# Expert selections in pieces, one to a slot of rows, and one head further ahead

## The chip, the cores and the metric

The kernel runs on one core of a Trainium2 chip. The metric is the device time of one execution in microseconds; lower is better. TensorE (PE) multiplies, VectorE (DVE) and ScalarE (ACT) do elementwise work, GpSimd (POOL) issues the indirect DMAs that gather rows by index, and SyncE (SP) issues the loads of weights. Each engine works through its own queue in order.

## What is computed

A two-layer diffusion backbone on 256 latent and 256 context tokens, 1024 wide, float32. Each layer has a token mixer (projections, windowed and differential attention, convolution, pooling, four gated branches) and then a feed-forward part that looks up experts (PEER). The change touches only the second:

```
q  = (h @ wq)                                  # 128 tokens, 8 heads, 2 x 128
s1, s2 = q[:, :, 0] . k1, q[:, :, 1] . k2      # 128 scores each
v1, i1 = top_k(s1, 16);  v2, i2 = top_k(s2, 16)
cand   = v1[:, None] + v2[None, :]             # 16 x 16 sums
sc, ci = top_k(cand, 16)
idx    = i1[ci // 16] * 128 + i2[ci % 16]      # 16 of 16384 experts
gate   = softmax(sc)
act    = gelu(sum_d h * u_tab[idx])
out    = sum over 8 heads, 16 experts: gate * act * v_tab[idx]
```

For each tile of 128 tokens that is 8 heads x 16 slots, and each slot fetches one row of u_tab and one of v_tab for each token: 128 x 1024 floats, 0.5 MB, twice. The last layer needs only the latent tiles, so there are six tiles to gather: layer 0 context tile 0, latent tiles 2 and 3, context tile 1, then layer 1 latent tiles 2 and 3.

## The kernel before

The kernel is written with a tile framework. Its build has a scheduler: the order in which the Python code writes instructions is their priority, and the scheduler puts an instruction into its engine's queue when, by its own estimates, its inputs and its buffers are ready and the engine is free. A lower priority can so pass a higher one that isn't ready yet. The queues are fixed when the kernel is built.

`gather(t, on_dve, nxt, side)` is a generator that does one tile. It has nine rounds `h` of 16 slots `k`. A slot issues `u_slot` (row of u for head `h`, line 1124 on POOL; product and sum on DVE, line 1132) and `v_slot` (row of v for head `h - 1`; added up on DVE, line 1149, or on TensorE, line 1156, with a diagonal made by ACT). A round ends with `weigh(h)`: Gelu on ACT (line 1138) and a product with the gate on DVE (line 1139). Row places are rings: five tiles for u, five for v, and more that `lend` adds where other buffers are free.

`select` finds the 16 experts of one head for one or two tiles (jobs): `top16` of each half of the scores (lines 1011 to 1015), the sums `cand` (1040), `top16` of these, the softmax (Exp on ACT, line 1049), the lookup through `df` (1060) and `pk` (1063), and `idx` (1064). Its tiles mx, ix, cand, sv, ci, pk have one buffer each. `route` is what comes before: it loads the head's w_q (1 MB, a ring `w` of three places that all weights share, line 231) and kt (one place), multiplies (line 218, then 1196 for the scores) and has ACT copy the scores to `sc` (1199).

`router` yields once for each head. `gather` takes one step of `side` ahead of each round, so that head `h + 1` is routed and selected, in one go, ahead of the slots of round `h`. Three gathers have such a `side`:

- the first gather (context tile 0, POOL issues from 410 to 985 us) runs `behind` the main work on the latent tiles; `pump` puts slots between the main work's pieces at fixed rates. Its side is `router((0, 1), ...)`, one tile per selection; the scores of tile 1 are written to `later` in DRAM.
- the second gather (tile 2, 1001 to 1404) runs alone, with `router((2, 3), ...)`, two tiles per selection.
- the third gather (tile 3, 1405 to 1782) runs alone, with `waited`, which reads the scores of tile 1 back and selects two heads at a time.

The fourth gather (context tile 1, 1784 to 2257) runs behind layer 1's main work and has no side. The fifth (2376 to 2783) begins behind the last of it and has `routes` as its side, which yields twice and then does heads 3 to 7; heads 0 to 2 are routed in the main code. The sixth (2784 to 3149) runs alone.

## Time and profile before

| | |
|---|---|
| median of 3 runs | 3176.56 us (3165.32 to 3186.99) |
| the profiled execution | 3168.74 us, span 3167.0 us |
| TensorE busy | 2376.9 us (75%) |
| VectorE busy | 2357.8 us (74%) |
| GpSimd busy | 1789.3 us (56%) |
| ScalarE busy | 654.6 us (21%) |
| read from HBM | 1032.22 MB, 327 GB/s over the span |

A share of the span is an average over the six gathers and the main work. Which engine or which transfers set the pace is to be read stretch by stretch. A wait is put down to what was released last; where that engine had long been done, it was something else, often the release of a buffer.

### The profile page before, as it was taken

What the parts mean: (1) busy time and instruction counts of PE and PEld (TensorE: products, weight loads), DVE (VectorE), ACT (ScalarE), POOL (GpSimd) and SP (SyncE); (2) the same over time, 40 slices, a digit from 0 to 9 for tenths busy, and PEclk for the clock granted to TensorE, in tenths of its full rate; (3) what the DMA queues carried; (4) which work ended last, traced back from release to release, by engine and by line L of the source; (5) the groups of instructions that cost most, each with busy time, mean ns of one, the idle gap of its engine ahead of it and who ended that gap; (6) DMA issues with size and microseconds to landing.
All of it is one profiled execution on the core that took longest, in us unless ns stands there. A gap on an engine that the chain in (4) does not pass through costs nothing.

```text
span 3167.0 us, 32196 instructions
## 1 busy us (share of the span) xinstructions
PE 2376.9 (75%) x10264; PEld 1586.2 (50%) x10264; DVE 2357.8 (74%) x5204; ACT 654.6 (21%) x1543; POOL 1789.3 (56%) x1542
## 2 busy tenths in 40 slices
PE   7999989898877785665455589899997966645555
PEld 5879878666666452222111267667696522211111
DVE  5977679678968899747666769977567985566666
ACT  3454321233112211110000211123332211100001
POOL 0000057443556687776777757766205777777775
PEclk9999999899988897886777789899998988876767
DMA  9948979787999899998999999999838989999998
GB/s 305 334 161 285 304 263 351 270 296 250 339 331 356 321 392 364 336 381 294 373 369 369 338 343 389 341 388 386 300 107 288 323 324 372 372 344 372 383 377 300
DMA packets 397863, 1036.48 MB, mean 327 GB/s; under 512 B 30464, under 2 KB 169216, under 8 KB 397696
## 3 DMA queue, kind: packets, MB, share of 16 engines
q0 software_dynamic: 221184, 805.40, 68.0%
q1 hardware_dynamic: 173072, 226.25, 21.0%
q10 hardware_dynamic: 3440, 2.78, 0.3%
q8 instruction: 82, 1.34, 0.2%
q14 instruction: 85, 0.70, 0.1%
HBM read 1032.22 MB, written 2.10 MB: 327 GB/s over the span
## 4 chain that ended last, share of the span: by engine, by line
PE 33%; DVE 18%; issue 17%; DMA 15%; POOL 15%; ACT 1%; another core or an unknown queue 0%; POOLq 0%; SPq 0%; ACTq 0%; DVEq 0%
PE mm L218 11%; POOL u L1124 8%; POOL v L1124 7%; DMA v<-in_v_dram,idx 7%; DVE u L1132 5%; PE va L1156 4%; DMA w<-in_w_gate_dram 3%; PE mm L214 3%; PE mm L216 2%; PE mm L215 2%; PE mm L916 2%; DMA u<-in_u_dram,idx 2%; DVE dacc L1149 2%; PE at L531 2%; DVE m L832 2%
## 5 line engine op out<-in xcount | busy, mean ns | idle before, releaser
L1124 POOL DMA_INDIRECT u<-in_u_dram,idx x768 | 869.7, 1132 | 926.4 <-DVE m L862 409.0
L1156 PE MATMUL va<-v,dg 128*128 128x512 f32 x1436 | 890.5, 763 | 554.5 <-DMA v<-in_v_dram,idx 379.8
L1132 DVE SCALAR_TENSOR_TENSOR u<-u,h 128x1024 f32<-128x1024 f32 x768 | 933.2, 1219 | 338.1 <-DMA u<-in_u_dram,idx 307.6
L1124 POOL DMA_INDIRECT v<-in_v_dram,idx x768 | 919.1, 1197 | 433.6 <-issue 193.9
L1156 PEld LDWEIGHTS va<-v,dg 128*128 128x128 f32 x1436 | 315.8, 237 | 1070.4 <-issue 925.6
L1149 DVE SCALAR_TENSOR_TENSOR dacc<-v,wt,dacc 128x1024 f32<-128x1024 f32 x403 | 515.6, 1279 | 105.9 <-DMA v<-in_v_dram,idx 78.6
L218 PE MATMUL mm<-hT,w 128*128 128x256 f32 (+1 forms) x1664 | 383.4, 385 | 71.4 <-DMA w<-in_w_gate_dram 50.9
L218 PEld LDWEIGHTS mm<-hT,w 128*128 128x128 f32 x1664 | 312.4, 207 | 130.2 <-issue 53.6
L1154 ACT ACTIVATE dg<-ident,wt 128x128 f32<-128x128 f32 x359 | 141.3, 400 | 1029.9 <-PE va L1156 524.7
L832 DVE SCALAR_TENSOR_TENSOR m<-m,cols,m 128x256 f32<-128x256 f32 x360 | 158.2, 473 | 0.1
L916 PE MATMUL mm<-hT,w 128*128 128x256 f32 x512 | 134.5, 405 | 14.5 <-DVE t L453 6.6
L215 PE MATMUL mm<-hT,whi 128*128 128x256 f32 x512 | 143.4, 280 | 0.0
L214 PE MATMUL mm<-hT,whi 128*128 128x256 f32 x448 | 128.0, 286 | 3.1 <-ACT whi L176 3.1
L216 PE MATMUL mm<-hT,whi 128*128 128x256 f32 x448 | 127.2, 284 | 1.8 <-DVE whi L177 1.8
L218 PE MATMUL mm<-w,hT 128*128 128x256 f32 x512 | 117.1, 388 | 10.6 <-DMA w<-in_w_in_dram 10.6
L916 PEld LDWEIGHTS mm<-hT,w 128*128 128x128 f32 x512 | 97.6, 202 | 34.5 <-issue 17.2
L177 DVE TENSOR_TENSOR whi<-w,whi 128x1024 fp32r<-128x1024 f32 x86 | 103.6, 1220 | 13.8 <-ACT whi L176 6.5
L218 PEld LDWEIGHTS mm<-w,hT 128*128 128x128 f32 x512 | 99.1, 195 | 26.4 <-issue 12.5
L176 ACT CAST whi<-w 128x1024 fp32r<-128x1024 f32 x86 | 87.4, 1047 | 51.3 <-PE mm L216 20.6
L215 PEld LDWEIGHTS mm<-hT,whi 128*128 128x128 f32 x512 | 97.0, 190 | 0.4 <-issue 0.3
L214 PEld LDWEIGHTS mm<-hT,whi 128*128 128x128 f32 x448 | 85.3, 190 | 8.8 <-ACT whi L176 4.2
L216 PEld LDWEIGHTS mm<-hT,whi 128*128 128x128 f32 x448 | 84.8, 189 | 7.2 <-DVE whi L177 3.7
(361 smaller groups left out, 2960.9 us busy)
## 6 DMA issues: line engine op xcount, KB each, us to landing
w<-in_w_gate_dram SPq DMA_DIRECT2D x48, 1024.0 KB
w<-in_w_in_dram SPq DMA_DIRECT2D x42, 1024.0 KB
X<-in_w_mod_dram SPq DMA_DIRECT2D x40, 512.0 KB
wm<-in_w_mod_dram SPq DMA_DIRECT2D x40, 512.0 KB
w<-in_w_branch_dram SPq DMA_DIRECT2D x20, 1024.0 KB
w<-in_w_q_dram SPq DMA_DIRECT2D x20, 1024.0 KB
u<-in_u_dram,idx POOLq DMA_INDIRECT x768
v<-in_v_dram,idx POOLq DMA_INDIRECT x768
```

What stands on the lines that cost most here:

```text
L177: nc.vector.tensor_tensor(lo.bitcast(FR), v, hi, op=OP.subtract)
L214: nc.tensor.matmul(ps, ah, bh, start=first, stop=False)
L215: nc.tensor.matmul(ps, ah, bl, start=False, stop=False)
L216: nc.tensor.matmul(ps, al, bh, start=False, stop=last)
L218: nc.tensor.matmul(ps, a[:, kb, ca], b[:, kb, cb], start=first, stop=last)
L832: nc.vector.scalar_tensor_tensor(acc[:, b, :], yb[:, b, k:k + T], cols[:, l, cw + k:cw + k + 1], acc[:, b, :], op0=OP.mult, op1=OP.add)
L916: nc.tensor.matmul(ps, a[:, kb, ca], b[:, k0 + kb, cb], start=f, stop=z, skip_group_check=True)
L1124: nc.gpsimd.indirect_dma_start(out=r, out_offset=None, in_=table, in_offset=bass.IndirectOffsetOnAxis(ap=self.idx[:, j:j + 1], axis=0))
L1132: nc.vector.scalar_tensor_tensor(r, r, 1.0, self.h2, op0=OP.mult, op1=OP.mult, accum_out=self.act[:, j % 16:j % 16 + 1])
L1149: nc.vector.scalar_tensor_tensor(self.dacc, v, w, self.dacc, op0=OP.mult, op1=OP.add)
L1154: nc.scalar.activation(dg, ident, AF.Copy, scale=w)
L1156: nc.tensor.matmul(self.va[:, half, :], dg, v[:, half * 512:(half + 1) * 512], start=j == self.pe[0], stop=j == self.pe[-1])
```

## The change

`select`, `route` and `waited` become generators that yield 0 after a piece and 1 at the end of a head. `gather` takes steps until the first 1 ahead of round 0 (that is head 1), and then one step ahead of each slot until the next 1; what a round has not used up is done at its end. So round `h` now selects head `h + 2`. `at_once` runs a generator through where the selection is done in one go as before. For two tiles a head has ten steps, for one tile seven. In `routes` head 3 is done at once, in round 1; its `lend` follows as soon as a head is done.

```
 def select(jobs, scs):
...
         for j, sc in enumerate(scs):
             for b in range(2):
                 top16(sc[:, b * 128:(b + 1) * 128], mx[:, 2 * j + b], ix[:, 2 * j + b])
+                yield 0
...
         for j in range(J):
             top16(cand[:, j].rearrange("p a b -> p (a b)"), sv[:, j], ci[:, j])
+            yield 0
...
+        yield 0
         nc.vector.tensor_reduce(pk, df, axis=AX.X, op=OP.min, apply_absolute_value=True)
...
 def route(ts, l, h, hT, c0, later=None, w=None):
...
+        yield 0
+        yield 0
         if jobs:
-            select(jobs, scs)
+            yield from select(jobs, scs)
+
+    def at_once(steps):
+        for _ in steps:
+            pass
...
 def router(tiles, l, ts, later=None, beside=None):
...
             if i == 0:
-                route(ts[:1], l, 0, hT, 0, later)
+                at_once(route(ts[:1], l, 0, hT, 0, later))
...
         for h in range(1, 8):
-            route(ts, l, h, hT, 0, later)
+            yield from route(ts, l, h, hT, 0, later)
             yield 1
-        route(ts[1:], l, 0, hT, 128, later)
+        yield from route(ts[1:], l, 0, hT, 128, later)
         yield 1
...
 def waited(t, later):
...
-            select([(t, h), (t, h + 1)], scs)
+            yield from select([(t, h), (t, h + 1)], scs)
...
 def gather(t, on_dve, nxt=None, side=()):
...
         side = iter(side)
         t.begin(on_dve)
+        while not next(side, 1):
+            pass
         for h in range(9):
-            next(side, None)
             if h == 8:
                 t.gates()
+            over = False
             for k in range(16):
+                if not over:
+                    over = next(side, 1)
                 if h < 8:
                     t.u_slot(h * 16 + k)
                 if h > 0:
                     t.v_slot(h * 16 - 16 + k)
                 yield 1
+            while not over:
+                over = next(side, 1)
             if h < 8:
                 t.weigh(h)
...
         for h in range(3, 8):
-            route(tsl, 1, h, hT, 0, w=wq[h] if h < len(wq) else None)
+            steps = route(tsl, 1, h, hT, 0, w=wq[h] if h < len(wq) else None)
+            if h == 3:
+                at_once(steps)
+            else:
+                yield from steps
             lend(**freed.get(h, {}))
             yield 1
```

The other calls of `route` in layer 1's main code are wrapped in `at_once`.

## Rows read from the trace of the kernel before

**Rows 1.** Busy time of each engine in stretches, TensorE clock, DMA share, GB/s.

```profile
core 0: us, PE busy (x) PEld busy (x) DVE busy (x) ACT busy (x) POOL busy (x), PEclk, DMA share, GB/s
395.00:985.00 590.00, 505.60 (x2358) 411.79 (x2358) 479.05 (x1072) 134.46 (x318) 317.82 (x256) 0.92 0.86 306
420.00:550.00 130.00, 119.14 (x556) 102.68 (x554) 121.86 (x265) 18.89 (x39) 91.53 (x66) 0.97 0.92 329
550.00:985.00 435.00, 364.56 (x1676) 289.60 (x1677) 342.55 (x748) 106.37 (x252) 220.47 (x185) 0.90 0.85 306
1097.00:1303.00 206.00, 145.28 (x387) 74.06 (x385) 205.42 (x685) 36.60 (x86) 163.16 (x134) 0.84 0.98 369
1493.00:1764.00 271.00, 145.52 (x193) 46.64 (x192) 178.81 (x247) 20.46 (x54) 207.41 (x193) 0.72 0.98 372
1500.00:1550.00 50.00, 25.67 (x36) 8.58 (x36) 35.33 (x51) 3.03 (x8) 38.11 (x40) 0.78 1.03 407
2484.00:2590.00 106.00, 81.23 (x263) 46.18 (x263) 105.58 (x334) 22.64 (x53) 77.03 (x65) 0.90 0.89 314
```

**Rows 2.** Line 1064 in three stretches: count, ns, first and last start.

```profile
L1064 DVE SCALAR_TENSOR_TENSOR idx<-pk x8: 156/165/168, 409.1 to 875.1; 128x16 int32<-128x16 f32 x8
...
L1064 DVE SCALAR_TENSOR_TENSOR idx<-pk x13: 163/186/221, 1000.7 to 1295.3; 128x32 int32<-128x32 f32 x11, 128x16 int32<-128x16 f32 x2
...
L1064 DVE SCALAR_TENSOR_TENSOR idx<-pk x10: 154/175/228, 2375.1 to 2589.7; 128x32 int32<-128x32 f32 x6, 128x16 int32<-128x16 f32 x4
```

**Rows 3.** Line 1139, ends of the second gather's eight rounds, 990 to 1400.

```profile
L1139 DVE TENSOR_TENSOR wt<-wt,gate x8: 152/168/176, 1055.7 to 1389.2; 128x16 f32<-128x16 f32 x8
```

**Rows 4.** POOL in order of time; in brackets idle time before, and releaser.

```profile
451.83 1.86 POOL L1124 DMA_INDIRECT v<-in_v_dram,idx  x1 [7.54 <-DVE idx L1064]
...
507.75 1.68 POOL L1124 DMA_INDIRECT u<-in_u_dram,idx  x1 [3.94 <-DVE idx L1064]
...
584.60 0.93 POOL L1124 DMA_INDIRECT u<-in_u_dram,idx  x1 [1.55 <-DVE idx L1064]
...
1047.09 1.68 POOL L1124 DMA_INDIRECT u<-in_u_dram,idx  x1 [17.68 <-DVE idx L1064]
```

**Rows 5.** Waits of DVE for scores, 400 to 1000, then all: us, times, longest.

```profile
DVE mx L1011 <- ACT sc L1199: 10.8, 5, 5.1
...
DVE mx L1011 <- ACT sc L1199: 19.5, 9, 5.1
```

**Rows 6.** Waits of PE for weights, 400 to 1000.

```profile
PE mm L218 <- DMA w<-in_w_gate_dram: 50.9, 9, 13.6
...
PE mm L218 <- DMA w<-in_w_q_dram: 10.2, 3, 6.9
```

**Rows 7.** PE in order of time: one route of the first gather.

```profile
550.24 8.83 PE L218 MATMUL mm<-hT,w 128*128 128x256 f32 x32 [2.92 <-DMA w<-in_w_q_dram]
558.91 0.39 PE L1196 MATMUL mm<-kt,qT 128*128 128x128 f32 x2
...
559.54 0.94 PE L1196 MATMUL mm<-kt,qT 128*128 128x128 f32 x6
```

**Rows 8.** Chain that ended last, 540 to 700, its longest landings: start, us.

```profile
547.35 19.19 DMA w<-in_w_gate_dram
...
675.56 15.26 DMA w<-in_w_q_dram
```

**Rows 9.** Exp (line 1049), Gelu (line 1138) and their table loads.

```profile
L1049 ACT ACTIVATE gate<-gate x31: 198/228/232, 406.8 to 2583.5; 128x32 f32<-128x32 f32 x17, 128x16 f32<-128x16 f32 x14
L1049 ACT ACT_TABLE_LOAD  x13: 1283/1283/1283, 448.6 to 2582.1; - x13
...
L1138 ACT ACTIVATE wt<-act x48: 198/216/218, 448.3 to 3131.6; 128x16 f32<-128x16 f32 x48
L1138 ACT ACT_TABLE_LOAD  x21: 1283/1283/1283, 442.4 to 2625.1; - x21
```

**Rows 10.** The page's first part: busy us, share, instructions.

```profile
PE 2376.9 (75%) x10264; PEld 1586.2 (50%) x10264; DVE 2357.8 (74%) x5204; ACT 654.6 (21%) x1543; POOL 1789.3 (56%) x1542
```

More of the change, by code (lines that the diff above doesn't have):

```diff
@@ L1037, in select @@
                 top16(sc[:, b * 128:(b + 1) * 128], mx[:, 2 * j + b], ix[:, 2 * j + b])
+                yield 0
         cand = sb.tile([128, 2, 16, 16], F, tag="cand", name="cand", bufs=1)[:, :J]
@@ L1045, in select @@
             top16(cand[:, j].rearrange("p a b -> p (a b)"), sv[:, j], ci[:, j])
+            yield 0
         g, st = entries(t0.gates_, jobs), st8()
@@ L1062, in select @@
                                 op=OP.subtract)
+        yield 0
         nc.vector.tensor_reduce(pk, df, axis=AX.X, op=OP.min, apply_absolute_value=True)
@@ L1204, in route, with at_once @@
             scs.append(sc)
+        yield 0
+        yield 0
         if jobs:
-            select(jobs, scs)
+            yield from select(jobs, scs)
+    def at_once(steps):
+        for _ in steps:
+            pass
     def router(tiles, l, ts, later=None, beside=None):
@@ L1215, in router @@
             if i == 0:
-                route(ts[:1], l, 0, hT, 0, later)
+                at_once(route(ts[:1], l, 0, hT, 0, later))
                 if beside:
@@ L1221, in router @@
         for h in range(1, 8):
-            route(ts, l, h, hT, 0, later)
+            yield from route(ts, l, h, hT, 0, later)
             yield 1
-        route(ts[1:], l, 0, hT, 128, later)
+        yield from route(ts[1:], l, 0, hT, 128, later)
         yield 1
@@ L1232, in waited @@
                 nc.scalar.dma_start(sc, later[h + i])
-            select([(t, h), (t, h + 1)], scs)
+            yield from select([(t, h), (t, h + 1)], scs)
             yield 1
@@ L1240, in gather @@
         t.begin(on_dve)
+        while not next(side, 1):
+            pass
         for h in range(9):
-            next(side, None)
             if h == 8:
                 t.gates()
+            over = False
             for k in range(16):
+                if not over:
+                    over = next(side, 1)
                 if h < 8:
@@ L1250, in gather @@
                 yield 1
+            while not over:
+                over = next(side, 1)
             if h < 8:
@@ L1532, in body @@
     norm_T((2,), 1, 1, hT, 0)
-    route(tsl[:1], 1, 0, hT, 0, w=wq[0])
+    at_once(route(tsl[:1], 1, 0, hT, 0, w=wq[0]))
     tsl[0].prepare(True)
@@ L1544, in routes @@
         for h in range(3, 8):
-            route(tsl, 1, h, hT, 0, w=wq[h] if h < len(wq) else None)
+            steps = route(tsl, 1, h, hT, 0, w=wq[h] if h < len(wq) else None)
+            if h == 3:
+                at_once(steps)
+            else:
+                yield from steps
             lend(**freed.get(h, {}))
@@ L1552, in body @@
     lend(u=["ys1"])
-    route(tsl[:1], 1, 1, hT, 0, w=wq[1])
+    at_once(route(tsl[:1], 1, 1, hT, 0, w=wq[1]))
     out_proj(accT[:, :, cut(1)], (3,), 1, wout)
     norm_T((3,), 1, 1, hT, 128)
-    route(tsl, 1, 2, hT, 0, w=wq[2])
+    at_once(route(tsl, 1, 2, hT, 0, w=wq[2]))
     for h in range(2):
-        route(tsl[1:], 1, h, hT, 128, w=wq[h])
+        at_once(route(tsl[1:], 1, h, hT, 128, w=wq[h]))
         lend(**freed[h])
```

## Prediction

> **What bounds the kernel now.** I read the table of stretches first [rows 1], because the page's shares average over six gathers that have different limits. The reader is to see three kinds of stretch. Where a gather runs alone (1493 to 1764 us, third gather, no selection left) DVE is 66% busy, TensorE 54%, the DMA engines 98%, at 372 GB/s: the rows of the tables set the pace. Where a gather runs with selections beside it (1097 to 1303, second gather) DVE is busy for 205.42 of 206 us, but the DMA still moves 369 GB/s, so a DVE that is full costs almost nothing there. In 2484 to 2590 (fifth gather) DVE is full too and the DMA falls to 314 GB/s. The first gather (395 to 985) runs behind the main work: TensorE 86%, DVE 81%, DMA 86%, 306 GB/s; nobody is full and everybody waits for somebody. So the places to look at are the first gather and those 106 us of the fifth.
>
> Then I read when the selections are really done. The line that writes idx has a row for each [rows 2]: 8 between 400 and 985, 13 between 1000.7 and 1295.3, 10 between 2375.1 and 2589.7. Of the 13, four belong to the third gather's `waited`, whose rows begin only after the second gather's eighth round, which ends at 1389.2 [rows 3]. Program order is thus only a priority: the build's scheduler has already pulled the selections of the second, third and fifth gathers rounds ahead of where they are written, and mixed them with the rows. In the first gather it has not: there a head's idx arrives when its first row is wanted. That decides most of what follows.
>
> **The change part by part.** It adds and removes no device instruction: the same 31 selections, 48 weighings and 5204 DVE instructions [rows 10]. It moves priorities.
>
> *One head further ahead, first gather.* Before, head h+1 is routed at the start of round h; after, head h+2. GpSimd waited for idx four times [rows 4]: 7.54 us (head 1), 3.94 (head 2), 1.55 (head 3), and 17.68 us for head 1 of the second gather. Head 1 is routed before round 0 in both kernels, so 7.54 and 17.68 stay. Heads 2 and 3 get a round of slack: 3.94 + 1.55 = 5.5 us go. What is next late there is the release of one of five row places by DVE, so I count half, -2.7 us; ends 0 and -5.5.
>
> *Selections in pieces, with two empty slots after the route.* DVE executes in order; in five places of 400 to 1000 it stood idle for scores that ScalarE had not yet copied, 10.8 us; in the whole kernel nine times, 19.5 us [rows 5]. Behind such a stop stand the main work's products and the row products that free row places. Two slots between scores and first top-16 put other work ahead of it. With DVE at 81% in this stretch, about half of that is on the path: -5.4 us; ends 0 and -10.8. The last piece of a head comes seven slots into its round in the first gather (one tile) and ten in the others (two tiles), of 16, and is wanted a round later: nobody waits for it, and if it slips by six slots there is still a whole round of cover.
>
> *What the route brings with it.* A moved selection takes its 1 MB of w_q, its kt load and its matmuls along. One route on TensorE is 8.83 us of q products and 0.39 + 0.94 of scores [rows 7], 10.2 us. One such route moves out of 550 to 985 into 420 to 550, past SP's weight queue. TensorE is 119.14 of 130 us busy in the one and 364.56 of 435 in the other [rows 1], so the cost is 10.2 x (0.92 - 0.84) = +0.8 us if idle time absorbs in proportion; at worst all 10.2, with nothing back. For the load: TensorE waited 50.9 us for w_gate and 10.2 us (three times) for w_q [rows 6], and in the chain single landings take 15 to 19 us [rows 8]. One w_q fewer among them is 10.2 / 3 = -3.4 us; the ends are -10.2 (all three waits go) and +19.2 (the load lands in front of a weight that the main work wants, as the longest one did).
>
> *Second and third gather.* DVE full, DMA at 369 against 372 GB/s without selections: 206 x (1 - 369/372) = 1.7 us at most. I take 0. The Trainium skill speaks against any gain here: "DMA: Bandwidth & Descriptors", section Where 436 GB/s comes from, puts about 358 GB/s per core as what HBM to SBUF can give, and by it nothing is left at 369. The trace does not agree with the figure: 50 us of the third gather moved 407 GB/s [rows 1]. By that row up to 206 x (1 - 369/407) = 19 us could be had in the second gather, but the 271 us without any selection average 372, so I leave it out of the sum.
>
> *Fifth gather.* 106 us at 314 instead of 372 GB/s is 106 x (1 - 314/372) = 16.5 us of lost transfer time. The selections there are ten in 215 us, as closely packed as in the second gather; the change routes heads 3 to 7 a round earlier, head 3 at once, and hands back borrowed row places earlier. Nothing in it holds a piece back: a lower priority is passed over whenever the scheduler thinks that DVE is free, and by rows 2 it thought so rounds ahead. I take 0; ends -16.5 and +5, the 5 being an h = 3 selection that now precedes round 1's rows.
>
> *ScalarE's tables.* The 31 Exp cost 13 table loads and the 48 Gelu 21, 1283 ns each [rows 9]. There is still one Exp group and one Gelu in a round, so 0; at worst the other 18 Exp take a load each, 18 x 1.283 = 23 us on an engine that is 21% busy, of which only those just ahead of a weighing are on the path. The Trainium skill, "ScalarE: Activation LUTs", section What ACT_TABLE_LOAD costs, charges about 2.66 us for a switch, load and drain together; by it this bound would be 48 us. The rows show the 1283 ns; the drain I can't separate.
>
> *Sum.* -2.7 - 5.4 + 0.8 - 3.4 = -10.7, about -11 us. The profiled execution took 3168.74 us (span 3167.0); the median of the runs is 7.8 us above it, so the forecast is 3168.7 - 10.7 = 3158 in that execution's terms, 3166 as a median. The runs before spread by 22 us, 0.7%; about 1% (32 us) is what a measurement of this kernel can tell from no change.
>
> **The rivals.**
>
> *Nothing moves.* The scheduler had already taken selections out of written order [rows 2], so the new order gives nearly the same queues, and the waits for idx were only the last of several. For it: the four early `waited` selections. Against it: rows 4 and 5 show that in the first gather they were not early. Time 3177.
>
> *A larger gain.* All of the first gather's waits go (5.5 + 10.8), w_q leaves the path (10.2), and in the fifth gather the pieces really spread over the rounds (16.5): 43 us, 3134. For it: 314 GB/s with DVE full is just what spreading would mend. The Trainium skill, "Perfetto Trace Analysis", section Optimizing Scalar/DVE Operations, says that breaking work up helps where the vector engine isn't saturated but makes others wait. By that rule the first gather (81%) gains and the two full stretches do not, which is less than this rival asks for. Against it: nothing in the change keeps the scheduler from packing the selections again.
>
> *Slower.* The first gather starts with two routes in a row and every later w_q is one round earlier in the ring of three weight places. If TensorE, 92% busy from 420 to 550, passes the 10.2 us on, and one main weight then lands as late as 19.2 us, the main work is 29 us late; the gather's slots are tied to it by fixed rates and give nothing back: 3206. It decides as soon as the extra w_q displaces a weight that TensorE reaches before it lands. Against it: TensorE has 70 us of idle time after 550.
>
> **How the numbers follow.** Forecast (-11 us, with its own spread of some 15) 0.40; nothing moves 0.18; larger gain 0.25; slower 0.17. The likeliest gives 3166. The range takes the larger gain with some room below it, since its unknowns are bounds from both sides (3128), and reaches to just short of the slower case (3203). Faster by over 1%: most of the larger gain and the forecast's lower tail, 0.30. Slower by over 1%: the slower case ends at 0.9%, so some half of it and a rest for an order that comes out badly, 0.14. Within 1%: 0.56.
>
> **What would show it.** Right, if in the changed profile GpSimd's waits on idx in 400 to 1000 shrink from 13 us to the 7.5 of head 1, DVE's on the scores from 10.8 to near 0, the eighth idx of the first gather comes most of a round earlier than 875.1, and the first gather ends some 10 us sooner, with the stretches after it as long as now. Wrong, if the first gather keeps its length (then the waits were only exchanged, for row places or weights), if TensorE's wait for w_gate grows past 50.9 us (the slower rival), or if the fifth gather's full stretch is gone and the DMA there reaches 370 GB/s (the larger gain). The sum also fails if the scheduler, given other priorities, orders stretches anew that the change doesn't touch.

## The result, and the profile after

The changed kernel takes 3183.16 us (median of 20 runs, 3170.96 to 3200.02) against 3161.12 us of the kernel before (20 runs): a ratio of 1.0071, 95% interval 1.0053 to 1.0089, 22 us slower. The forecast was 11 us faster. Two later comparisons of the same instructions gave 1.0008 (0.9985 to 1.0031) and 1.0116 (1.0059 to 1.0173, six runs); the experiments come back to that.

The profiled execution took 3175.77 us, span 3173.4. First the page's busy line, then the stretches of [rows 1] in the changed kernel (same columns):

```profile
PE 2354.6 (74%) x10264; PEld 1577.6 (50%) x10264; DVE 2359.8 (74%) x5204; ACT 648.6 (20%) x1539; POOL 1787.5 (56%) x1542
```

```profile
395.00:985.00 590.00, 482.19 (x2239) 392.96 (x2240) 467.42 (x1055) 123.73 (x295) 294.13 (x248) 0.89 0.85 302
420.00:550.00 130.00, 119.91 (x567) 103.68 (x566) 120.97 (x286) 21.30 (x44) 77.75 (x63) 0.97 0.92 324
550.00:985.00 435.00, 341.37 (x1556) 270.30 (x1555) 331.55 (x704) 92.79 (x224) 211.49 (x181) 0.87 0.84 301
1097.00:1303.00 206.00, 137.09 (x389) 70.32 (x387) 198.84 (x652) 38.13 (x88) 165.42 (x131) 0.88 0.97 359
1493.00:1764.00 271.00, 141.38 (x192) 45.82 (x191) 177.90 (x246) 20.05 (x53) 201.37 (x192) 0.71 0.98 373
2484.00:2590.00 106.00, 83.38 (x270) 48.71 (x271) 104.67 (x326) 23.15 (x53) 86.14 (x66) 0.91 0.92 332
```

The work is the same (as many DVE instructions, busy 2359.8 us against 2357.8 in [rows 10]). In 550 to 985 less of it gets done: TensorE 341.37 us against 364.56, DVE 331.55 against 342.55, and what is missing is done later. So the loss shows as idle time in the first gather. From its first row to the first row of the second gather it takes 610.6 us (413.6 to 1024.1) against 591.0 (410.2 to 1001.2), which is nearly the whole 22. (The two profiled executions as a whole lie only 6.4 us apart, since the third gather took 366.8 us in place of 378.0 in this one and the fourth 586.0 in place of 592.6. That the loss belongs to the first gather is settled below, by runs.) The stretch 2484 to 2590 moves 332 GB/s in place of 314, but from the fifth gather's first row to the sixth's it is 407.1 us against 408.0.

What the change was to do, it did in part. The line that writes idx, in the three stretches of [rows 2]:

```profile
L1068 DVE SCALAR_TENSOR_TENSOR idx<-pk x8: 156/166/170, 412.4 to 806.4; 128x16 int32<-128x16 f32 x8
...
L1068 DVE SCALAR_TENSOR_TENSOR idx<-pk x13: 154/178/201, 1023.7 to 1318.9; 128x32 int32<-128x32 f32 x11, 128x16 int32<-128x16 f32 x2
...
L1068 DVE SCALAR_TENSOR_TENSOR idx<-pk x10: 163/172/190, 2380.7 to 2588.2; 128x32 int32<-128x32 f32 x6, 128x16 int32<-128x16 f32 x4
```

The eighth idx comes at 806.4 us, a round earlier than 875.1. The second and fifth gathers' idx come as densely as before. Of GpSimd's waits for idx [rows 4] those for heads 2 and 3 (3.94 and 1.55 us) are gone. Up to 1060 us the profile names idx as the releaser of no row any more, but two waits for it are still there under other names. The 17th u row of a gather is the first of head 1, and it can't go before head 1's idx is written (changed kernel, first and second gather, DVE's line above GpSimd's):

```profile
456.17 0.16 DVE L1068 SCALAR_TENSOR_TENSOR idx<-pk 128x16 int32<-128x16 f32 x1
...
456.60 0.94 POOL L1128 DMA_INDIRECT u<-in_u_dram,idx  x1 [11.86 <-DVE wt L1143]
...
1061.20 0.18 DVE L1068 SCALAR_TENSOR_TENSOR idx<-pk 128x32 int32<-128x32 f32 x1
...
1061.64 0.94 POOL L1128 DMA_INDIRECT u<-in_u_dram,idx  x1 [10.13 <-DVE mx L1011]
```

Both rows start 0.27 us after the end of idx, as the rows at 507.75, 584.60 and 1047.09 us of the kernel before do (0.27 to 0.28). The fourth wait of [rows 4], 7.54 us, was probably none for idx: the row behind it is a v row of head 0, which doesn't read head 1's idx, and it starts 0.27 us after the end of the first product on v, which frees a v place (kernel before):

```profile
450.82 0.74 DVE L1147 TENSOR_SCALAR dacc<-v,wt 128x1024 f32<-128x1024 f32 x1
```

And here is what else changed, waits of TensorE and of DVE in the changed kernel, 400 to 1000 us (us in total, times, longest):

```profile
PE mm L218 <- DMA w<-in_w_gate_dram: 68.0, 8, 14.8
PE tr L803 <- DVE st L360: 9.2, 1, 9.2
PE mm L218 <- issue: 6.9, 1, 6.9
PE mm L1200 <- DMA kt<-in_kt_dram: 6.4, 1, 6.4
```

```profile
DVE th L941 <- PE mm L218: 29.6, 6, 13.1
DVE st L846 <- PE tr L796: 14.7, 1, 14.7
DVE mx L1011 <- ACT sc L1203: 7.4, 3, 4.5
```

The three waits for w_q (10.2 us, [rows 6]) are gone, though a route now waits once for kt, its other load. Two waits of TensorE for v rows (13.9 us in the kernel before) are gone too. The waits for w_gate grew from 50.9 to 68.0 us, DVE's for the branch products (line 941) from 19.3 to 29.6, and there are new or longer waits around lines 796 to 856 (DVE's at line 846 was 1.9 us). Those lines are the convolution branch of the main work: 120 steps on DVE (line 832), a statistic on TensorE (796) and its copy (838), a broadcast (803), a second statistic (796, 846) and broadcast, then ys (856), which the last quarter of the gated branches needs.

The place where it shows is the order in TensorE's queue there. Kernel before (start, us, tile and shape, idle time before):

```profile
842.37 1.17 PE L796 MATMUL tr<-few_cols,m 128*128 128x1 f32 x10
...
844.35 0.61 PE L803 MATMUL tr<-ident,st 128*128 128x128 f32 x4
844.79 3.19 PE L218 MATMUL mm<-hT,w 128*128 128x256 f32 x14
847.82 1.84 PE L796 MATMUL tr<-few_cols,m 128*128 128x1 f32 x16
...
857.19 0.71 PE L803 MATMUL tr<-ident,st 128*128 128x128 f32 x4 [0.50 <-DVE sc L1013]
863.66 6.37 PE L218 MATMUL mm<-hT,w 128*128 128x256 f32 x16 [5.76 <-DMA w<-in_w_gate_dram]
869.87 1.89 PE L218 MATMUL mm<-ys,w 128*128 128x256 f32 x8
871.60 3.62 PE L218 MATMUL mm<-hT,w 128*128 128x256 f32 x16
```

The changed kernel:

```profile
862.07 1.17 PE L796 MATMUL tr<-few_cols,m 128*128 128x1 f32 x10
...
864.04 0.61 PE L803 MATMUL tr<-ident,st 128*128 128x128 f32 x4
...
875.97 2.90 PE L218 MATMUL mm<-hT,w 128*128 128x256 f32 x6 [10.03 <-DMA w<-in_w_gate_dram]
878.66 3.41 PE L796 MATMUL tr<-few_cols,m 128*128 128x1 f32 x16
...
895.32 1.19 PE L803 MATMUL tr<-ident,st 128*128 128x128 f32 x4 [9.24 <-DVE st L360]
903.40 3.78 PE L218 MATMUL mm<-ys,w 128*128 128x256 f32 x8 [6.89 <-issue]
```

Before, all four steps of the conv pass ahead of the gate product that waits for its w_gate. After, the second statistic stands behind it in an in-order queue: TensorE idles 10.03 us for the weight, the statistic comes at 878.66, DVE has meanwhile stood 14.73 us in front of it with the rows' products queued behind, and TensorE then waits for DVE (9.24). Its next wait of 6.89 us has no releaser in the profile, but ends within 0.1 us of the writing of ys (902.1 to 903.3 us, against 862.5 to 863.7 before).

The main work's gate tanh (ACT, line 902; 32 of them from 570 us on) tell what each stop costs. The 20th starts 3.9 us later than in the kernel before, the 21st 18.2, the 25th 16.1, the 26th 36.6 and the last 37.8 (960.8 against 923.0). So there are two stops: about 14 us at the w_gate issued near 815 us, between the 20th and the 21st, and about 20 at the conv, between the 25th and the 26th. The first row of the second gather comes 23.0 us later, so some 15 of the 37.8 are made up behind the main work; 3.4 of the 23.0 are the first gather's own late start.

Such a stop also costs on the way out. In the first of the two, TensorE did nothing for 14.85 us (a stretch of it in the changed kernel, columns as above):

```profile
820.00:830.00 10.00, 0.00 (x0) 0.00 (x0) 9.27 (x16) 0.00 (x0) 6.49 (x7) 0.53 1.04 394
```

The granted clock is 0.53 there, near the lower of its two levels (1.2 of 2.4 GHz), and 0.50 in the 5 us after it. In the kernel before, the products after the 5.76 us stop take 6.37 us (granted clock 0.57), the next of their shape 3.62 (1.00).

### The profile page after: what moved, and what is told of

It reads as the page before. It is cut to its first block, busy times and chain, and to the rows that moved or that the text cites. A ratio compares the mean times of both kernels' runs of the same rounds, so it can differ in the third digit from the quotient of the medians.

```text
span 3173.4 us, 32197 instructions
## 1 busy us (share of the span) xinstructions
PE 2354.6 (74%) x10264; PEld 1577.6 (50%) x10264; DVE 2359.8 (74%) x5204; ACT 648.6 (20%) x1539; POOL 1787.5 (56%) x1542
## 4 chain that ended last, share of the span: by engine, by line
PE 31%; issue 18%; POOL 16%; DVE 16%; DMA 15%; ACT 1%; another core or an unknown queue 1%; POOLq 0%; SPq 0%; ACTq 0%; DVEq 0%
PE mm L218 9%; POOL v L1128 8%; POOL u L1128 8%; DMA v<-in_v_dram,idx 7%; DVE u L1136 5%; PE va L1160 4%; DMA w<-in_w_gate_dram 3%; DMA u<-in_u_dram,idx 3%; PE mm L214 3%; PE mm L216 2%; PE mm L215 2%; DVE dacc L1153 2%; PE mm L916 2%; PE at L531 2%; DVE m L832 2%
## 5 line engine op out<-in xcount | busy, mean ns | idle before, releaser
L1128 POOL DMA_INDIRECT u<-in_u_dram,idx x768 | 884.0, 1151 | 947.2 <-DVE m L862 412.4
L1160 PE MATMUL va<-v,dg 128*128 128x512 f32 x1436 | 869.8, 749 | 557.2 <-DMA v<-in_v_dram,idx 386.8
L1128 POOL DMA_INDIRECT v<-in_v_dram,idx x768 | 902.9, 1176 | 420.3 <-issue 198.8
```

Source lines behind the costliest of these rows:

```text
L1128: nc.gpsimd.indirect_dma_start(out=r, out_offset=None, in_=table, in_offset=bass.IndirectOffsetOnAxis(ap=self.idx[:, j:j + 1], axis=0))
L1160: nc.tensor.matmul(self.va[:, half, :], dg, v[:, half * 512:(half + 1) * 512], start=j == self.pe[0], stop=j == self.pe[-1])
```

## The experiments

The theories at first: **1**, the head further ahead costs (its extra route and w_q at the start of the first gather); **2**, the pieces cost (selection work now lies between the main work's steps on DVE); **3**, any new order moves this stretch by some 20 us, and the change just drew a bad one. Later ones are told where they arise. All variants are the changed kernel with two switches for each gather, and with both off it is the kernel before, instruction for instruction:

```
+    def head(side):
+        while not next(side, 1):
+            pass
-    def gather(t, on_dve, nxt=None, side=()):
+    def gather(t, on_dve, nxt=None, side=(), ahead=True, pieces=True):
...
-        while not next(side, 1):
-            pass
+        if ahead:
+            head(side)
         for h in range(9):
+            if not pieces:
+                head(side)
...
-            over = False
+            over = not pieces
```

All results in one table. The ratio is to runs of the kernel before on the same chip (their median beside it). The length of the first gather is from its first row to the second gather's first row. The ys lag is from the start of the 24th gate tanh (line 902) to the end of line 856; the next column is TensorE's wait for w_gate, 395 to 1035 us. The last is the time from SP's issue of the pair of w_gate near 815 us to the product that waited for it, with the rows that GpSimd had issued in the 10 us before (a dash where TensorE's wait there is put down to something else or there is none). The first gather and the three last columns are from one profiled execution each. The ratios come from 12 runs each, but for 20 of after and six each of h_before and as_after_2.

| kernel | ratio (before) | first gather | ys lag | w_gate wait | issue to product (rows) |
|---|---|---|---|---|---|
| before | (3161) | 591.0 | 22.4 | 50.9 | 5.3 (2) |
| as_before | 0.9995, 0.996 to 1.003 (3102) | 588.4 | 22.4 | 49.6 | 5.3 (2) |
| e3_not_first | 0.9977, 0.9951 to 1.0003 (3170) | 591.7 | 22.4 | 50.8 | 5.2 (2) |
| e7_later_pieces | 0.9957, 0.9931 to 0.9983 (3189) | 596.7 | 22.4 | 59.3 | 5.3 (2) |
| e7_again | 0.9960, 0.9931 to 0.9990 (3193) | 603.4 | 22.4 | 59.7 | 5.6 (4) |
| c1_rate | 0.9992, 0.9958 to 1.0026 (3102) | 594.6 | 22.4 | 51.6 | - |
| e1_pieces | 1.0008, 0.998 to 1.0036 (3170) | 609.7 | 27.9 | 62.5 | 9.5 (4) |
| e5_first_pieces | 1.0024, 0.9987 to 1.0061 (3102) | 603.0 | 27.1 | 56.1 | - |
| e2_ahead | 1.0029, 1.0003 to 1.0055 (3170) | 590.5 | 31.7 | 52.9 | 12.4 (4) |
| e6_first_ahead | 1.0029, 1.0 to 1.0057 (3102) | 600.3 | 32.8 | 53.4 | - |
| after | 1.0071, 1.0053 to 1.0089 (3161) | 610.6 | 47.8 | 68.0 | 16.5 (7) |
| e4_only_first | 1.0055, 1.0026 to 1.0085 (3170) | 612.1 | 47.8 | 71.6 | 16.0 (7) |
| as_after | 1.0008, 0.9985 to 1.0031 (3193) | 611.5 | 48.3 | 66.3 | 16.9 (7) |
| as_after_2 | 1.0116, 1.0059 to 1.0173 (3085) | 608.5 | 48.2 | 68.3 | 15.5 (7) |
| c3_rate_after | 1.0068, 1.0039 to 1.0097 (3189) | 615.0 | 36.7 | 71.0 | 7.6 (3) |
| c4_after_conv | 1.0042, 1.0006 to 1.0078 (3104) | 595.9 | 5.3 | 69.3 | 10.7 (5) |
| c5_before_conv | 1.0054, 1.0016 to 1.0092 (3104) | 614.9 | 10.0 | 66.7 | - |
| e8_late_start | 1.0086, 1.005 to 1.0122 (3104) | 621.7 | 46.5 | 68.8 | 14.6 (5) |
| h_before | 0.9889, 0.9845 to 0.9934 (3189) | 567.1 | 22.4 | 31.3 | - |
| h_after | 0.9946, 0.9916 to 0.9976 (3189) | 582.9 | 41.0 | 48.0 | 13.1 (7) |

**Which gather, which half.** e1: `pieces` on, `ahead` off, in all gathers with a side. e2: the other way round. e3: both off in the first gather, on in the others. e4: both on in the first gather only.

> The selections of all four gathers that have them are handed out in pieces, one to a slot of rows, but one head is routed ahead as in the kernel before, not two. Theory 1 (the loss is the extra route and the extra w_q at the start of the first gather, whose main work then meets its w_gate late): no loss here, ratio 0.995 to 1.002, TensorE's wait for w_gate in 395 to 1030 near the 51 us of before, the second gather's first row products near 1001 us. Theory 2 (the loss is the pieces: DVE work of selections now lies between the main work's statistics): the whole loss is here, ratio 1.005 to 1.009, start of the second gather near 1024. Theory 3 (any new order of the first gather moves this stretch by some 20 us either way): no prediction of the sign, and the size doesn't add up over the four runs.

> One head further ahead in all four gathers, but each selection is done in one go at the start of its round. Theory 1: the whole loss, ratio 1.005 to 1.009, the first gate tanh of the stretch some 10 us later than the 573 us of before, start of the second gather near 1024. Theory 2: 0.998 to 1.002, second gather near 1001. Theory 3: anything between 0.993 and 1.01.

> The first gather as in the kernel before; the second, third and fifth with pieces and one head further ahead. Theory 1 and 2 both: the first gather ends as before (start of the second near 1001 us); what is left is the effect of the change on the later gathers. In the changed kernel's trace the third gather's first round gave back some 17 us of a delay of 23; if that is a gain of the change's own in the later gathers, this kernel is faster than before, ratio 0.994 to 0.997; if it was only slack that a late start fills, 0.999 to 1.002.

> Only the first gather with pieces and one head further ahead; the others as in the kernel before. Theory 1 and 2: start of the second gather near 1024 us; if the later gathers' 17 us were the change's own gain, the ratio is 1.007 to 1.012 (more than the whole change's 1.007); if they were slack, 1.002 to 1.007. Theory 3: the start of the second gather lands elsewhere, by over 8 us, though the first gather's code is the same as in the changed kernel.

e3 and e4 place it: with the first gather alone changed the kernel is slower by 0.55%, with all others changed it is not (0.9977). The halves don't separate here: by the ratio e1 speaks for theory 1, by its first gather (609.7 us) for theory 2, and e2 is the reverse, with a first gather of 590.5 and a ratio of 1.0029. One execution can't decide, so the same was asked of the first gather alone (e5 pieces, e6 ahead), with two controls: the kernel before with another slot rate, and itself.

```
-    MR, RATE0, RATE1, RATE2 = 1.01, (1.023, 0.887, 0.823, 1.018, 0.972), 1.325, 0.753
+    MR, RATE0, RATE1, RATE2 = 1.01, (1.023, 0.887, 0.823, 1.03, 0.972), 1.325, 0.753
```

> Only the first gather changed, and only by the pieces; one head ahead as before. Theory 2 (pieces): the second gather starts 15 to 25 us later than the 1001 us of before and the ratio is 1.003 to 1.008. Theory 1 (the head further ahead): start 997 to 1005, ratio 0.998 to 1.002. A fourth theory, from the four runs so far: neither half costs by itself as much as both together; the pieces cost some 10 us and the head ahead nothing to the rows, though main work falls 12 us back there; then the start is 1010 to 1022 and the ratio 1.000 to 1.004.

> Only the first gather changed, and only by routing one head further ahead, each selection in one go. Theory 1: start of the second gather near 1024 us, ratio 1.003 to 1.008. Theory 2: 997 to 1005, ratio 0.998 to 1.002. Fourth theory: rows ahead of before (the eighth weighing near 965 us instead of 971), the last gate tanh of the stretch 8 to 15 us late because w_gate lands behind more rows, and the two cancel at the start of the second gather: 995 to 1005, ratio 0.998 to 1.003.

> The kernel before with one rate of the first gather's slots, the fourth of the list of five, at 1.03 in place of 1.018. A control for theory 3 (any other order of this stretch moves it by some 20 us): by theory 3 the second gather's start moves by 8 us or more either way and the ratio lies outside 0.998 to 1.002. By the others: start within 5 us of 1001, ratio within 0.998 to 1.002.

> The code of the changed kernel with both halves switched off in every gather: the kernel before, instruction for instruction in the same order on every engine. A second execution of it under the profile. Ratio 0.998 to 1.002. If the spread of one kernel's executions is a drift of the rows' transfers, the first gather and its main work come out as before to within 3 us (second gather's start 998 to 1008) and the differences lie in the last gather, which ran 382.8 us to the end in the kernel before, and 384 to 395 in the others though its code is the same.

Each half seems to cost something, 0.24% and 0.29%, and the two together e4's 0.55%; but neither by itself is clear of no change here, and e6's second gather starts at 1011.9 us, where none of its theories had it. In the first gather's length the pieces (609.7, 603.0) stand near both together (608.5 to 612.1, four executions), the head ahead (590.5, 600.3) within those of the old first gather (588.4 to 603.4, five). c1 speaks against theory 3 in its crude form, since it cost nothing (0.9992); but it is a weak control, for it touched rates late in the stretch only, and its ys lag and its waits for w_gate are those of the kernel before. What doesn't vary at all from execution to execution is the ys lag: 22.4 us in every kernel with the old first gather, 27 to 28 with pieces, 32 to 33 with the head ahead, 48 with both. So it goes with the order in the queues and not with the execution.

**Rows in front of weights, or the order.** In the table's last column the same weight takes 5.2 or 5.3 us behind two rows, 5.6 to 12.4 behind four, and behind seven 15.5 to 16.9 (13.1 in h, where some of the rows are cut). Rows go out in bursts (in the changed kernel ten from 803.8 to 817.5 us, after 8.9 us of waiting for a row place), and a weight that SP issues then comes late. So the **rows theory**: this lateness is the loss. Against it the **order theory**: the steps of the conv stand where two engines stop on each other. h cuts the u rows in rounds 3 to 6 of the first gather, in both kernels (the products then run on stale data, scaled down by a factor that the code below leaves out); c3 holds rows back before 815 us by a slot rate. e7 asks another question, which half is the better one in the later gathers.

```
             if j % 16 == 0:
                 self.act = sb.tile([128, 16], F, tag="act", name="act", bufs=3)
-            r = self.row(u_d, "u", j)
+            if self.l == 0 and self.t == 0 and 48 <= j < 112:
+                r = self.kept[j % 5]
+                nc.gpsimd.indirect_dma_start(out=r[:, :128], out_offset=None,
+                                             in_=u_d.rearrange("r (a c) -> (r a) c", c=128),
+                                             in_offset=bass.IndirectOffsetOnAxis(ap=self.idx[:, j:j + 1], axis=0))
+            else:
+                r = self.kept[j % 5] = self.row(u_d, "u", j)
...
```

c3, in the changed kernel:

```
-    MR, RATE0, RATE1, RATE2 = 1.01, (1.023, 0.887, 0.823, 1.018, 0.972), 1.325, 0.753
+    MR, RATE0, RATE1, RATE2 = 1.01, (1.023, 0.887, 0.78, 1.018, 0.972), 1.325, 0.753
```

e7 (the third and the fifth like the second):

```
-    behind.append(gather(tsc[0], P_C0, None, rc))
+    behind.append(gather(tsc[0], P_C0, None, rc, ahead=False, pieces=False))
...
-    every(gather(tsl[0], P_L0, tsl[1], rl))
+    every(gather(tsl[0], P_L0, tsl[1], rl, ahead=False, pieces=True))
```

> The kernel before, but in rounds 3 to 6 of the first gather the rows of the first table (u) are cut from 1024 to 128 columns, 4 KB to 512 bytes each; the row products keep their size, on data that stay from earlier rows, scaled by 1/16. To be compared with the same cut in the changed kernel, not with the kernel before. Here TensorE's wait for the w_gate that it needs near 816 us, 2.7 us before, stays below 3 us, and the second gather starts at 975 to 1003 us.

> The changed kernel with the same cut of the u rows in rounds 3 to 6 of the first gather. Rows theory (a w_gate lands late because more rows went out just ahead of it: in ten kernels so far 2 to 3 rows in the 10 us before its issue go with a wait of 2.6 us on TensorE, 4 with 7 to 10, 7 with 14 to 15): with a third less to move, that wait falls from 14.9 to under 7 us, and against the same cut in the kernel before the last gate tanh is 3 to 15 us late instead of 38, the start of the second gather 0 to 10 us instead of 20, the ratio between the two kernels under 1.004. Order theory (the conv's statistics and the gate blocks stand in an order that stops TensorE and DVE on each other, whatever the rows weigh): the last gate tanh stays 25 to 40 us late, the second gather's start 15 to 25, the ratio 1.005 to 1.009.

> The changed kernel with one rate of the first gather's slots lowered, the third of five, 0.823 to 0.78, so that fewer slots of rows are handed out from about 690 to 790 us. Rows theory: fewer rows stand in front of the w_gate pair issued near 815, TensorE's wait there falls below 10 us and part of the 20 us comes back: ratio 1.001 to 1.005. If the rate doesn't reach the order in which rows go out: 1.005 to 1.009, and the wait stays at 14 to 15 us.

> The first gather as in the kernel before; the second, third and fifth with pieces but one head ahead as before. If pieces are what helps in the later gathers (from the start of the second to the end the profiled execution with pieces everywhere took 13 us less than before, the one with the head ahead everywhere 14 us more, of which 12.6 in the last gather, whose code is the same): ratio 0.994 to 0.998. If nothing in the later gathers is more than the spread of single executions: 0.998 to 1.002.

The rows theory fails as the whole cause. With the cut, both first gathers are some 25 us shorter, but the changed one is still 15.8 us longer than the other (19.6 without the cut), the last gate tanh 43.5 us later (935.7 against 892.1), and the w_gate waits differ by 16.7 us as before (17.1). The runs say the same: 0.9946 over 0.9889 is 1.0058, within the 1.005 to 1.009 that the order theory gave (the gate tanh is later than its 25 to 40 us). In c3 the wait near 815 did shrink, from 14.85 to 5.12 us, and came back at the next two weights, where the changed kernel waits 10.03 and 13.96 us (TensorE of c3, in order of time):

```profile
822.10 6.48 PE L218 MATMUL mm<-hT,w 128*128 128x256 f32 x16 [5.12 <-DMA w<-in_w_gate_dram]
872.53 5.18 PE L218 MATMUL mm<-hT,w 128*128 128x256 f32 x16 [14.20 <-DMA w<-in_w_gate_dram]
924.37 5.89 PE L218 MATMUL mm<-hT,w 128*128 128x256 f32 x13 [18.45 <-DMA w<-in_w_gate_dram]
```

The sum of the waits stayed (71.0 us) and so did the ratio, 1.0068. A late weight is real, but making one of them punctual gave nothing back here.

**The conv's place.** In all kernels so far with a new first gather the main work's 26th gate tanh starts 7.6 to 8.6 us after ys, whenever that comes: it follows ys. In those with the old one it is 5.5 to 14.9 us, and what ends the wait is mostly a weight. So the **conv theory**. c4 hands out the conv's pieces faster in the changed kernel, c5 does the same in the kernel before:

```
-    T2 = (2.319, 1.61, 1.125)
+    T2 = (2.319, 1.85, 1.125)
```

e8 tests theory 1's remainder, that the extra route at the start is what is passed on: it moves it to round 3 (no step of the side in round 0, one more head at once in round 3 of the first gather).

```
             if not pieces:
                 head(side)
+            if h == 3 and t.l + t.t == 0:
+                head(side)
...
-            over = not pieces
+            over = not pieces or (h == 0 and t.l + t.t == 0)
```

> The changed kernel with the conv's pieces handed out faster in the stretch before the one where they end (1.85 pieces to a gate block in place of 1.61), so that conv's last steps and its two statistics come about two gate blocks earlier. Conv theory (the conv's result is what the main work waits for, since DVE and TensorE reach its statistics late and stop on each other there): ys is done under 30 us after the 24th gate tanh instead of 47.8, the last gate tanh is at 925 to 942 instead of 960.8, the second gather starts at 1001 to 1012 instead of 1024, ratio 0.998 to 1.003. If the conv is only late with everything else: start 1018 to 1030, ratio 1.005 to 1.009.

> The kernel before with the same faster conv. Conv theory: there ys is not what the main work waits for last (5.6 to 11.7 us lie between it and the next block, and w_gate's landing ends the wait), so the time stays: ratio 0.998 to 1.002, start of the second gather 998 to 1010. If the earlier conv helps or hurts by itself, whatever the routes do, it does so here too.

> The changed kernel, but in the first gather the extra route is taken in round 3 (at once, at its start) and not in round 0, with one head ahead in pieces until then. Extra-route theory (the 10 us of the extra route on a TensorE that is 92% busy at the start are passed on): the first gate tanh is back at 572 to 577 us from 582.9, the second gather starts at 1008 to 1014, ratio 1.002 to 1.005. Conv theory: the first gate tanh comes back too, but ys stays 40 us or more behind the 24th gate tanh and the second gather starts at 1016 to 1028, ratio 1.005 to 1.009.

c4 does in its trace what the conv theory asked: the statistics and broadcasts pass ahead of the product that waits, the ys lag is 5.3 us, the last gate tanh at 931.8 in place of 960.8, the first gather 595.9 us. TensorE in c4:

```profile
829.02 1.17 PE L796 MATMUL tr<-few_cols,m 128*128 128x1 f32 x10
...
835.33 1.84 PE L796 MATMUL tr<-few_cols,m 128*128 128x1 f32 x16
...
848.34 0.61 PE L803 MATMUL tr<-ident,st 128*128 128x128 f32 x4
...
875.19 5.14 PE L218 MATMUL mm<-hT,w 128*128 128x256 f32 x12 [16.65 <-DMA w<-in_w_gate_dram]
```

It waits for w_gate as long as the changed kernel (69.3 us), but its 26th gate tanh starts 25.4 us earlier and its first gather is 15 us shorter. So in this one execution an earlier conv, with w_gate as late as ever, gives back 15 of the 20 us. (Executions of the old first gather differ by as much, 588.4 to 603.4 us; those of the changed one don't, 608.5 to 612.1.) The time doesn't confirm it: 1.0042 is above the 1.003 expected, and its interval overlaps with the changed kernel's. And c5 went against me: the same edit makes the kernel before slower, 1.0054, its first gather 614.9 us, with an earlier conv that nobody waits for (the 26th gate tanh comes 26.6 us after ys) and 66.7 us of waits for w_gate. Its TensorE there:

```profile
851.49 1.84 PE L796 MATMUL tr<-few_cols,m 128*128 128x1 f32 x16
...
865.30 0.61 PE L803 MATMUL tr<-ident,st 128*128 128x128 f32 x4
...
887.99 2.47 PE L218 MATMUL mm<-hT,w 128*128 128x256 f32 x5 [13.15 <-DMA w<-in_w_gate_dram]
```

So one rate, moved by the same amount, shortens the first gather with one order and lengthens it with the other: theory 3 in a finer form. It suggests that the rates in the code go with the order of the kernel before. e8 refutes the extra route at the start: the first gate tanh is back at 574.5 us, but the ys lag is 46.5, the first gather the longest of all (621.7 us) and the ratio 1.0086. The extra route still comes, in round 3, so what it costs anywhere else in the gather is not excluded.

Two kernels of the table speak against the conv's place as the whole cause. In c3 the ys lag is 11 us smaller than in the changed kernel and the last gate tanh 14.3 us earlier (946.5), yet the first gather is no shorter, 615.0 us. In e1 the lag is only 27.9 and the last gate tanh at 936.1, and the first gather still takes 609.7. What lies between is the rows. After the last gate tanh GpSimd has this many rows of the first gather still to issue, and this long it takes until the second gather's first row:

| | before | e1 (pieces) | e2 (ahead) | after | c3 | c4 |
|---|---|---|---|---|---|---|
| rows left | 36 | 33 | 17 | 15 | 25 | 29 |
| us | 78.2 | 85.9 | 64.1 | 63.4 | 78.1 | 74.8 |

Rows go on while the main work stands, so a stop of the main work costs less than its length, and ending it earlier gives back less. How much of the 20 us is w_gate's, the conv's and the rows' is thus not settled.

**Once more.** e7 a second time and the changed kernel twice, to see what is steady.

> The kernel of e7 once more, on whatever chip: first gather as in the kernel before, pieces without the further head in the second, third and fifth. If the 0.9957 was real: 0.993 to 0.998. If it was the draw of that comparison: 0.998 to 1.002. The first gather takes 588 to 598 us in any case.

> The changed kernel, instruction for instruction, once more. Order theory (the length of the first gather follows from the order on the engines, hardly from the execution): ys 47 to 49 us after the 24th gate tanh as in the two executions of this first gather so far (47.8 both), TensorE's wait for the second w_gate of the pair near 815 us 14 to 15 us, the first gather 608 to 614 us long; ratio 1.004 to 1.009.

> The changed kernel a third time, instruction for instruction. The first gather is 608 to 614 us long, as in the three executions of it so far, with ys 47 to 49 us after the 24th gate tanh. If the loss of the whole kernel depends on the chip, the ratio may lie anywhere from 1.000 to 1.008; if the 1.0008 was a draw, 1.004 to 1.008.

The first gather of the changed kernel is nearly the same in all its executions, 608.5 to 612.1 us. The ratio of the whole is not: 1.0071, 1.0008, 1.0116, the first two with intervals that exclude each other, and as_after missed its 1.004. Each interval holds the runs of one comparison, on one chip, and the chips differ more. The third gather, alone and with the same rows, took 378.0 us from its first row to the fourth's in the profile of before (1405.6 to 1783.6) and 343.4 in as_before (1391.9 to 1735.2). In the profiles of the experiments it took 366 to 378 us on three chips and 335 to 351 on two others, whatever the variant. The chip isn't all, for on one of these two the kernel before had medians of 3104 and 3085 us in two comparisons. On the chip of the 1.0008 e7 ran in the same comparison at 0.9960, so there the new first gather and the head further ahead together cost some 15 us of 3193. Why the ratio of the whole differs between comparisons stays open. e7 is faster than the kernel before in both comparisons, by 0.4%, about 13 us, and faster than the changed kernel. Where it gains the traces don't show: its two profiled executions were the slowest, or nearly so, of its runs, and its first gather in the second came to 603.4 us, outside the 588 to 598 expected.

## Why the prediction was wrong

- **The step that failed** is what the moved route does to the weights: "one w_q fewer among them is 10.2 / 3 = -3.4 us", with +19.2 as its upper end. The waits for w_q did go, all 10.2 us (with one of 6.4 for kt in their place), but w_gate's grew by 17.1, to 68.0. The sum priced each moved instruction where it went and took the queue of the main work, in which it went there, as given. There was no term for that order; the last sentence of the prediction named it as what would break the sum, without a price or a chance. By the gate tanh the main work lost about 14 us where it waited for the w_gate near 815 us and about 20 where the conv's steps stood behind a product that waits (ys lag 47.8 for 22.4 us). Some 15 of the 37.8 us are made up by rows that went out meanwhile. That the loss sits in the first gather is shown by e3 and e4. That the conv's place is the larger part of it is not shown: c4 gave 15 of the 20 us back in one execution but not in its time, and c3 gave none. That c5, with the same edit, loses in the kernel before, with more waiting for w_gate, suggests that it is the order's doing as a whole.
- **Waits for idx**, -2.7: heads 2 and 3 went, 5.5 us, just as forecast, and head 1's stayed, as forecast: 11.86 and 10.13 us, under other names. (That 7.54 us was head 1's idx is probably a misreading.) The 5.5 us gave no time back: the first gather got longer. Half was too much.
- **Scores**, -5.4: wrong. 7.4 us in three waits are left of 10.8 in 400 to 1000 [rows 5]; two empty slots don't keep DVE from reaching the selection early, presumably since the scheduler places it by its own estimate.
- **The route on TensorE**, +0.8 (at worst 10.2): right. The first gate tanh is 9.8 us late (582.9 against 573.1) and the 20th only 3.9 (815.0 against 811.1), before the jump; the first gather's own start is 3.4 us late.
- **Second, third and fifth gathers**, 0: not contradicted by e3 (0.9977, 0.9951 to 1.0003), but the pieces alone gain 0.4% there (e7, twice), which the sum had at nothing. The higher rate in 2484 to 2590 that the larger gain hoped for came and bought nothing. **Tables**, 0: right, 30 loads for Exp and Gelu in place of 34 [rows 9].
- **The rivals.** "Slower" had the direction, the place, the sign of trouble (w_gate over 50.9 us) and nearly the size, and a main weight did come late, by 12.2 us near 815; but its reason, the extra w_q and route at the start, is refuted by e8. Its 0.17 was too little: the stretch has TensorE 86%, DVE 81% and DMA 86% busy, with the rows tied to the main work by fixed rates, and there a new order was more likely to hurt than to help. Of the ten experiments with another order in the first gather (e1, e2, e4, e5, e6, c1, c3, c4, c5, e8) nine came out at 1.0008 to 1.0086, six of them clear of no change, and c1 at 0.9992.

## What to carry to other kernels

Where several engines are each 80 to 90% busy and tied to each other by hand-set rates, a change of priorities is a change of every queue in the stretch: look first for short steps whose result a later stage needs (a statistic, a broadcast) and ask what could come to stand in front of them in an in-order queue, above all a product that waits for a load. Removing the wait that shows was worth little here, since the next one took its place (one w_gate for the next in c3); a price for "the order comes out otherwise" belongs in the sum, of the size of the stops that the stretch already has. Such rates may have to be set anew after the change (c4 and c5 point to it, though no run here regained the time that way). Confirm on more than one chip.

## What the runs showed of the hardware

A 1 MB weight issued by SP reached TensorE's product after 5.3 us with two rows issued in the 10 us before it and after 15.5 to 16.9 us with seven, in the same place of the program. The queues of the page, rows first, weights second (packets, MB, share of the engines):

```profile
q0 software_dynamic: 221184, 805.40, 68.0%
q1 hardware_dynamic: 173072, 226.25, 21.1%
```

From 820 to 830 us the DMA moved 394 GB/s, so 16.5 us for 1024 KB are 63 GB/s, a sixth of it. In those 16.5 us (814.99 to 831.53, changed kernel) the two queues moved:

```profile
q0 software_dynamic: 1363, 4.95, 76.5%
q1 hardware_dynamic: 1536, 1.56, 27.2%
```

So the weights' queue got 94 GB/s, 24% of the bytes: 1.05 MB for the weight that TensorE waited for, and 0.5 MB for the second of the pair, which SP had issued 1.7 us after the first. The Trainium skill, "DMA: Bandwidth & Descriptors", section Queues, rings and completion order, says that each DMA engine goes round the queues that have work and takes one packet from each in turn. By the mean packets of the whole page, 3641 and 1307 bytes, an estimate by that page would give the weights' queue 26%, 104 GB/s, and a weight alone in it a landing after 10 us. The trace agrees with the share (24%, and nearly as many packets of the one queue as of the other); the landing took longer because two weights shared it.
